# Loading the first tile of a Huber loss kernel in unequal groups of rows

## The chip, the core and the metric

The kernel runs on one core of a Trainium2 chip. Its time is the device time of one execution in microseconds (us); the time before is the median of three runs, 1868.19 us (1867.81 to 1869.9).

## The reference

Two arrays of 8192 x 8192 float32, `pred` and `target`, go in, and the elementwise Huber loss with delta 1 comes out as an array of the same shape.

```python
delta = 1.0
diff = pred - target
abs_diff = np.abs(diff)
return np.where(abs_diff <= delta, 0.5 * diff**2, delta * (abs_diff - 0.5 * delta))
```

The kernel computes it without a choice between branches: with d the difference and c = d clipped to [-1, 1], the loss is the larger of c * c / 2 and |d| - 1/2.

## The kernel before

Each array is taken as one flat row of numbers and cut into 40 blocks. A block is seen as 128 rows, one for each partition of the on-chip memory. `widths` gives the numbers in a row: 7616 in block 0, the remainder, and W = 13248 in the 39 others. `H`, `Q` and `E` are a half, a quarter and an eighth of W.

There are two pairs of buffers, `a_slots` for `pred` and `b_slots` for `target`; block i uses pair i % 2. The schedule is manual: the instructions of each engine stand in the order in which the code writes them. `load(0)` and `load(1)` come first; then, for each block, `compute(i)`, `store(i)` and `load(i + 2)`.

All loads and stores are issued by SyncE (SP in the profile, SPq where its sequencer is meant), so that they go through one queue in one order. In `load`, the inner function `get` (line 53) issues one DMA for some columns of all 128 rows. Blocks 0, 1, n - 3 and n - 2 are loaded in two halves of the columns, `pred` and `target` in turn; the last block in quarters; the others whole. For block 0 that is four DMAs of 128 x 3808 numbers, a row of each being 15232 bytes. `store` (line 70) writes a block from its b buffer, the last block in five pieces.

`compute` takes a block in pieces, block 0 in two halves. VectorE (DVE) subtracts into a (line 92) and clips into b (line 93); ScalarE (ACT) squares b, scaled (line 96), and takes the absolute value of a (line 97); DVE then takes the larger of a - 1/2 and b (line 86, in `finish`, which runs up to two pieces behind). The result stands in b, which `store` reads. So the next load into a buffer waits for ACT, and into b buffer for the store before it.

Of the kernel before, what the change touches and what calls it, by code (L numbers as in the profile page):

```python
# [1 line left out]

# [4 lines left out]


@with_exitstack
def kernel(  # L10
    ctx: ExitStack,
    tc: tile.TileContext,
    pred: bass.AP,
    target: bass.AP,
    out: bass.AP,
):
    nc = tc.nc
    P = 128
    fp32 = mybir.dt.float32
    Alu = mybir.AluOpType  # L20
    Act = mybir.ActivationFunctionType
    SQRT_HALF = 0.70710678118654752

    total = pred.shape[0] * pred.shape[1] // P
    W = 13248
    H, Q, E = W // 2, W // 4, W // 8

    widths = [W] * (total // W)
    if total % W:
        widths.insert(0, total % W)  # L30
    n = len(widths)
    starts = [sum(widths[:i]) * P for i in range(n)]

    def block(x, i):
        flat = x.rearrange("r m -> (r m)")
        return flat[starts[i] : starts[i] + P * widths[i]].rearrange("(p m) -> p m", p=P)

    pool = ctx.enter_context(tc.tile_pool(name="slots", bufs=1))
    a_slots = [pool.tile([P, W], fp32, name=f"a{k}") for k in range(2)]
    b_slots = [pool.tile([P, W], fp32, name=f"b{k}") for k in range(2)]  # L40

    def cuts(pieces):
        at, found = 0, []
        for w in pieces:
            found.append(slice(at, at + w))
            at += w
        return found

    def load(i):
        a, b = a_slots[i % 2], b_slots[i % 2]  # L50

        def get(dst, src, c):
            nc.sync.dma_start(out=dst[:, c], in_=block(src, i)[:, c])  # L53

        if i == n - 1:
            c = cuts([Q] * 4)
            order = [(0, 0), (0, 1), (1, 0), (1, 1), (0, 2), (1, 2), (0, 3), (1, 3)]
            for which, k in order:
                get((a, b)[which], (pred, target)[which], c[k])
            return  # L60
        w = widths[i]
        pieces = [w // 2] * 2 if i in (0, 1, n - 3, n - 2) else [w]
        for c in cuts(pieces):
            get(a, pred, c)
            get(b, target, c)

    def store(i):
        pieces = [Q] * 3 + [E] * 2 if i == n - 1 else [widths[i]]
        for c in cuts(pieces):
            nc.sync.dma_start(out=block(out, i)[:, c], in_=b_slots[i % 2][:, c])  # L70

    def compute(i):
        if i == n - 1:
            pieces = [E] * 8
        elif i == n - 2:
            pieces = [Q] * 4
        elif i == 0:
            pieces = [widths[0] // 2] * 2
        else:
            pieces = [W // 3] * 3  # L80
        todo = []

        def finish(keep):
            while len(todo) > keep:
                a, b = todo.pop(0)
                nc.vector.scalar_tensor_tensor(  # L86
                    out=b, in0=a, scalar=-0.5, in1=b, op0=Alu.add, op1=Alu.max
                )

        for c in cuts(pieces):  # L90
            a, b = a_slots[i % 2][:, c], b_slots[i % 2][:, c]
            nc.vector.tensor_tensor(out=a, in0=a, in1=b, op=Alu.subtract)  # L92
            nc.vector.tensor_scalar(  # L93
                out=b, in0=a, scalar1=-1.0, scalar2=1.0, op0=Alu.max, op1=Alu.min
            )
            nc.scalar.activation(out=b, in_=b, func=Act.Square, scale=SQRT_HALF)  # L96
            nc.scalar.activation(out=a, in_=a, func=Act.Abs)  # L97
            todo.append((a, b))
            finish(2)
        finish(0)  # L100

    ctx.enter_context(tc.manual_schedule())

    load(0)
    load(1)
    for i in range(n):
        compute(i)
        store(i)
        if i + 2 < n:
            load(i + 2)  # L110


# [1 line left out]
_INS = ['pred', 'target']  # L114
_OUTS = [((8192, 8192), 'float32')]


# [23 lines left out]
```

## Time and profile before

| what | value |
|---|---|
| median of 3 runs | 1868.19 us |
| profiled execution, its own time | 1869.17 us |
| its span in the profile | 1867.4 us |
| DVE busy | 1406.2 us, 75% |
| ACT busy | 903.9 us, 48% |
| DMA queue, share of 16 engines | 99.9% |
| bytes read and written | 536.87 MB and 268.44 MB, 431 GB/s over the span |
| DVE L92 waiting for `target` loads | 439.2 us in 42 waits |

The profile shows one execution. The span runs from the first instruction of the program to the last; the profiled execution's own time is 1.77 us longer. "L92" is line 92 of the kernel. A name such as b<-in_target_dram is what is written and what is read. The DMA share is the mean over the core's 16 DMA engines. An idle time in brackets, as in [12.55 <-DMA b<-in_target_dram], is how long the engine had nothing to run before the instruction, and what ended that.

### The profile page before, as it was taken

What the parts mean: (1) busy time and instruction counts of PE and PEld (TensorE: products, weight loads), DVE (VectorE), ACT (ScalarE), POOL (GpSimd) and SP (SyncE); (2) the same over time, 40 slices, a digit from 0 to 9 for tenths busy, and PEclk for the clock granted to TensorE, in tenths of its full rate; (3) what the DMA queues carried; (4) which work ended last, traced back from release to release, by engine and by line L of the source; (5) the groups of instructions that cost most, each with busy time, mean ns of one, the idle gap of its engine ahead of it and who ended that gap; (6) DMA issues with size and microseconds to landing.
All of it is one profiled execution on the core that took longest, in us unless ns stands there. A gap on an engine that the chain in (4) does not pass through costs nothing.

```text
span 1867.4 us, 994 instructions
## 1 busy us (share of the span) xinstructions
DVE 1406.2 (75%) x375; ACT 903.9 (48%) x251; POOL 0.2 (0%) x4
## 2 busy tenths in 40 slices
DVE  5677777777777777777777777777777777777886
ACT  3444444444444444444444444444444444444454
POOL 0000000000000000000000000000000000000000
DMA  9999999999999999999999999999999999999999
GB/s 412 423 432 436 436 431 433 436 432 431 428 435 434 435 432 432 432 435 434 434 434 435 432 434 432 435 434 432 436 434 432 434 434 432 432 436 430 432 429 390
DMA packets 19879, 805.37 MB, mean 431 GB/s; under 512 B 2208, under 2 KB 2208, under 8 KB 2464
## 3 DMA queue, kind: packets, MB, share of 16 engines
q1 hardware_dynamic: 19872, 805.32, 99.9%
q14 instruction: 7, 0.06, 0.0%
HBM read 536.87 MB, written 268.44 MB: 431 GB/s over the span
## 4 chain that ended last, share of the span: by engine, by line
DMA 61%; DVE 37%; issue 0%; SPq 0%; DVEq 0%
DMA b<-in_target_dram 33%; DMA out_dram<-b 28%; DVE b L86 15%; DVE a L92 15%; DVE b L93 8%; SPq L53 0%; DVEq L136 0%; DVEq L92 0%
## 5 line engine op out<-in xcount | busy, mean ns | idle before, releaser
L96 ACT ACTIVATE b<-b 128x4416 f32<-128x4416 f32 (+3 forms) x125 | 461.1, 3688 | 945.6 <-DVE b L93 945.6
L92 DVE TENSOR_TENSOR a<-a,b 128x4416 f32<-128x4416 f32 (+3 forms) x125 | 565.4, 4523 | 439.2 <-DMA b<-in_target_dram 439.2
L86 DVE SCALAR_TENSOR_TENSOR b<-a,b 128x4416 f32<-128x4416 f32 (+3 forms) x125 | 558.6, 4521 | 2.7 <-ACT a L97 2.7
L97 ACT ACTIVATE a<-a 128x4416 f32<-128x4416 f32 (+3 forms) x125 | 460.3, 3682 | 0.0
L93 DVE TENSOR_SCALAR b<-a 128x4416 f32<-128x4416 f32 (+3 forms) x125 | 293.1, 2344 | 4.3
L96 ACT ACT_TABLE_LOAD x1 | 1.3, 1283 | 0.7 <-PEq L125 0.7
L125 POOL MEMSET const-bfloat16-1.0<- 128x1 bf16 x1 | 0.1, 102 | 0.0
L125 POOL MEMSET const-uint8-127<- 128x1 uint8 x1 | 0.1, 101 | 0.0
L125 POOL MEMSET const-float32-0.0<- 128x1 f32 x1 | 0.1, 99 | 0.2 <-issue 0.2
L125 POOL MEMSET const-float32-1.0<- 128x1 f32 x1 | 0.1, 98 | 0.0
## 6 DMA issues: line engine op xcount, KB each, us to landing
out_dram<-b SPq DMA_DIRECT2D x38, 6624.0 KB, 26.9
a<-in_pred_dram SPq DMA_DIRECT2D x35, 6624.0 KB, 42.1
b<-in_target_dram SPq DMA_DIRECT2D x35, 6624.0 KB, 31.3
a<-in_pred_dram SPq DMA_DIRECT2D x6, 3312.0 KB, 30.4
b<-in_target_dram SPq DMA_DIRECT2D x6, 3312.0 KB, 30.5
a<-in_pred_dram SPq DMA_DIRECT2D x4, 1656.0 KB, 31.6
b<-in_target_dram SPq DMA_DIRECT2D x4, 1656.0 KB, 18.6
out_dram<-b SPq DMA_DIRECT2D x3, 1656.0 KB, 18.9
```

Source lines behind the costliest of these rows:

```text
L86: nc.vector.scalar_tensor_tensor(out=b, in0=a, scalar=-0.5, in1=b, op0=Alu.add, op1=Alu.max)
L92: nc.vector.tensor_tensor(out=a, in0=a, in1=b, op=Alu.subtract)
L93: nc.vector.tensor_scalar(out=b, in0=a, scalar1=-1.0, scalar2=1.0, op0=Alu.max, op1=Alu.min)
L96: nc.scalar.activation(out=b, in_=b, func=Act.Square, scale=SQRT_HALF)
L97: nc.scalar.activation(out=a, in_=a, func=Act.Abs)
L125: nc = _bacc.Bacc("TRN2", target_bir_lowering=False, num_devices=1)
```

## The change

The four DMAs of block 0 are each split by rows. The two of `pred` become DMAs of rows 0 to 111, 112 to 125 and 126 to 127; the two of `target` become DMAs of rows 0 to 111, 112 to 121 and 122 to 127. Columns, buffers, the order of the four column pieces, all other loads, the compute and the stores stay as they were. Twelve DMAs are issued in the place of four.

```diff
+    PRED_ROWS = (112, 14, 2)
+    TARG_ROWS = (112, 10, 6)
...
-        def get(dst, src, c):
-            nc.sync.dma_start(out=dst[:, c], in_=block(src, i)[:, c])
+        def get(dst, src, c, rows=(P,)):
+            r = 0
+            for m in rows:
+                nc.sync.dma_start(out=dst[r : r + m, c], in_=block(src, i)[r : r + m, c])
+                r += m
...
-            get(a, pred, c)
-            get(b, target, c)
+            get(a, pred, c, PRED_ROWS if i == 0 else (P,))
+            get(b, target, c, TARG_ROWS if i == 0 else (P,))
```

## The prediction

> **What bounds the kernel.** I read the engine table and the DMA lines of the page first, then the chain, the timeline of the first 60 us, and last the DMA share in the closing microseconds. From the page:
>
> ```profile
> DVE 1406.2 (75%) x375; ACT 903.9 (48%) x251; POOL 0.2 (0%) x4
> DMA 9999999999999999999999999999999999999999
> DMA packets 19879, 805.37 MB, mean 431 GB/s; under 512 B 2208, under 2 KB 2208, under 8 KB 2464
> q1 hardware_dynamic: 19872, 805.32, 99.9%
> DMA 61%; DVE 37%; issue 0%; SPq 0%; DVEq 0%
> ```
>
> No compute engine is near its limit. The DMA share is 9 in every one of the 40 slices, and the one queue's packets fill 99.9% of 16 engines. The program issues 138 DMAs of 128 rows each, and 138 x (128 + 16) = 19872: each row is one packet, and each DMA closes with 16 tiny packets (138 x 16 = 2208, the "under 512 B" count), one for each DMA engine. So an engine carries 8 rows of each DMA. The 37% of DVE in the chain is not a second bound: behind it the DMA queue is never empty. The kernel takes as long as the DMA engine that ends last needs for its own rows and stalls.
>
> The timeline shows the first tile:
>
> ```profile
> 0.73 0.37 SPq L53 DMA_DIRECT2D a<-in_pred_dram  x1
> 1.16 0.42 SPq L53 DMA_DIRECT2D b<-in_target_dram  x1
> ...
> 4.39 0.49 SPq L53 DMA_DIRECT2D b<-in_target_dram  x1
> 12.55 4.12 DVE L92 TENSOR_TENSOR a<-a,b 128x3808 f32<-128x3808 f32 x1 [12.55 <-DMA b<-in_target_dram]
> ...
> 21.62 4.13 DVE L92 TENSOR_TENSOR a<-a,b 128x3808 f32<-128x3808 f32 x1 [2.76 <-DMA b<-in_target_dram]
> ...
> 38.78 0.35 SPq L70 DMA_DIRECT2D out_dram<-b  x1
> ...
> 53.65 4.76 DVE L92 TENSOR_TENSOR a<-a,b 128x4416 f32<-128x4416 f32 x1 [7.73 <-DMA b<-in_target_dram]
> ```
>
> All eight loads are issued by 4.9 us. The two halves of the first tile become ready at 12.55 and 21.62, 9.07 us apart, and a half is two DMAs: 4.53 us for 128 rows, so an engine takes 4.53 / 8 = 0.567 us for a row of 15232 bytes. The first half would be in at 0.73 + 9.07 = 9.80 if the queue had been running; it came at 12.55, so starting from empty costs 2.75 us.
>
> The windows over the end (columns: stretch, length, DVE, ACT and POOL busy, clock, DMA share, GB/s):
>
> ```profile
> 1860.00:1862.00 2.00, 0.00 (x0) 0.00 (x0) 0.00 (x0) 1.00 0.97 401
> 1862.00:1863.00 1.00, 0.00 (x0) 0.00 (x0) 0.00 (x0) 1.00 0.61 252
> 1863.00:1864.00 1.00, 0.00 (x0) 0.00 (x0) 0.00 (x0) 1.00 0.43 179
> 1864.00:1865.00 1.00, 0.00 (x0) 0.00 (x0) 0.00 (x0) 1.00 0.27 113
> 1865.00:1866.00 1.00, 0.00 (x0) 0.00 (x0) 0.00 (x0) 1.00 0.10 40
> ```
>
> The 16 engines do not stop together: they run dry one after another over some 4 us. This unevenness is what uneven first loads could repair. The work left after 1862 is 0.61 + 0.43 + 0.27 + 0.10 = 1.41 us of all 16; shared perfectly it would end at about 1863.5, against about 1866.5 now. No redistribution of rows can gain more than about 3.0 us, or 0.16%.
>
> **The change, part by part.** Bytes, compute instructions and everything after the first tile stay. Four DMAs become twelve.
>
> *Rows per engine.* A 112-row DMA gives each of 16 engines 7 rows. If a small DMA gives an engine at most one row, an engine gets between 28 rows (none of the small ones) and 36 (one from each of the eight), against 32 before: from -4 x 0.567 = -2.3 us to +2.3 us. Which engines are late at the end the profile does not tell (it does not number them), so the sign for the last engine is open. [...]
>
> *Eight more issues on SP.* Each costs 0.37 to 0.65 us. In the built program the DMAs take eight landing semaphores in turn, so that issues 9 to 16 now each wait for the landing of issues 1 to 8; before, the eight initial loads waited for nothing. Behind the waiting issue on SP stand the rest of the first tile and the four loads of the second. When issue 9 waits for the first 112 rows, issues 2 to 8 are in the queue: at least 14 rows or 7.9 us for every engine, against about half a microsecond for an issue. I cost this at nothing; the cover is that backlog, and where it is gone a start from empty costs 2.75 us. Later waits find their semaphores long landed.
>
> *Compute.* DVE gets the first half later by whatever the loads lose. The first store is issued at 38.78 while queued loads last until 53.6: 14.9 us of cover. A loss in the loads moves both ends alike, so the cover stays, and the loss goes to the end of the program unchanged.
>
> *Rows 112 to 127 by themselves.* Here the trace has no row: every DMA of before spans 128 partitions of the tile. Now, four times, 16 neighbouring rows are written alone, by up to 14 engines at once. The lower bound is one row's time, 0.57 us, if the engines don't hinder each other. As the upper bound I take a full piece, 4.53 us, as if the set of 16 cost as much as 128. Likewise the 112 rows cost between 7/8 of a piece, 3.96 us, and a full one, if taking 16 rows off leaves some of what 16 engines write to idle. The sums are 4 x (3.96 + 0.57) = 18.1 us, no change, and 4 x (4.53 + 4.53) = 36.2 us, or +18.1. Nothing in the trace lies nearer to one end, so I take the middle: 4 x (4.53 + 2.27) = 27.2 us, +9.1 us. I don't take the lower end because packets of 16 engines running at one fixed pace, each on its own eight rows, say nothing of fourteen on one small block.
>
> [...]
>
> **The sum.** The profiled execution has a span of 1867.40 and a time of 1869.17, so 1.77 us lie around the span; it is 0.98 above the median 1868.19. Span after: 1867.40 + 9.1 = 1876.5; time 1878.3; median 1877.3.
>
> **Rivals.**
>
> *Evening out (not slower).* If engines don't hinder each other in those 16 rows, only the row counts matter. If the engines that end last are those that get 28 or 30 rows, the last loses 2.3 us, the next ones 1.1, and the early ones take the time over: about 1.9 us gained, 1866.3. If the late engines get the extra rows it is up to 2.3 us lost, 1870.5. It decides where a set of 16 rows costs less than about 1.1 us instead of 2.27. For it: each engine keeps to 0.567 us a row, and the tail of 4 us is of the size that plus or minus 2.3 us makes. Against it: the late engines would have to be the right ones. Either way it stays within 0.2% (3.7 us), which is about what a measurement of this kernel can tell from no change; a gain over that is excluded but for chance, since perfect balance gives 3.0.
>
> *Few rows are not spread.* If a small DMA runs on one or few engines, or 112 rows are spread badly, one engine gets up to 4 x 16 = 64 rows for its four: about +34 us, 1902; a milder case, +18, is the upper end of my own bounds, 1886. For it: only 128-row DMAs have been seen on 16 engines. Against it: 112 is a multiple of 16, and nothing forces the small sets together.
>
> *An empty queue.* The waits of issues 9 to 16 could let some engines run dry if engines drift apart by more than the 7.9 us of backlog. The engines that run dry are the early ones, which lose nothing at the end, so I put 2.75 us as its most, 1871, and little chance.
>
> **How the numbers follow.** Hindrance in the small sets, with +4 to +14 us around +9.1: 0.58. Evening out, within 0.2% either way: 0.26, of which 0.02 for a gain over 0.2%. Not spread: 0.10. A small loss, an empty queue among it, +2.3 to +4: 0.06, some 0.02 of it within 0.2%. So faster 0.02, same 0.26, slower 0.72. The range runs from 1866.6, which takes in most of the second case, to 1884, which takes in the first up to +16; some 0.05 is left out below and 0.12 above. The likeliest case alone has 1872 to 1882.
>
> **What would show it.** Right: the first DVE instruction starts about 4.5 us later (17 instead of 12.55), the second half about 9 us later (31), packets in the first 25 us last longer than one row's usual time and the GB/s of that stretch fall from about 435 to about 300, and from there everything is the old trace moved by 9 us, the tail of uneven engines longer than 4 us. Wrong: the two halves again about 9 us apart, the GB/s unchanged from 4 us on; then the only difference is in the closing microseconds, a steeper fall (gain) or a longer one (loss). If the halves are 9 us or more late each, rows are not spread.

## The result, and the profile after

The changed kernel takes 1885.87 us (median of 5 runs, 1885.58 to 1886.05), the kernel before 1868.15: 17.7 us more, a ratio of 1.0093 with a 95% interval of 1.0078 to 1.0108. The forecast was slower by 9.1 us with a range up to 1884.0, so the direction was right and the size half of the measured one. The profiled execution has a span of 1884.2 us.

From the page of the changed kernel:

```profile
DVE 1406.3 (75%) x375; ACT 903.9 (48%) x251; POOL 0.2 (0%) x4
DMA 9999999999999999999999999999999999999998
GB/s 258 438 434 432 434 432 433 434 434 434 434 433 436 433 433 433 433 433 433 435 434 432 434 434 432 434 436 433 432 435 434 432 434 433 434 433 427 424 423 383
DMA packets 19943, 805.37 MB, mean 427 GB/s; under 512 B 2272, under 2 KB 2272, under 8 KB 2528
q1 hardware_dynamic: 19936, 805.32, 99.8%
```

The compute is the same to 0.1 us. The DMA share is still 9 nearly everywhere, and this is the trap of this profile: the engines look just as busy. What changed is the rate, and nearly all of it in the first of the 40 slices: 258 GB/s, where the same line of the kernel before begins with 412:

```profile
GB/s 412 423 432 436 436 431 433 436 432 431 428 435 434 435 432 432 432 435 434 434 434 435 432 434 432 435 434 432 436 434 432 434 434 432 432 436 430 432 429 390
```

The share counts the time that packets take, however little they move in it: between 15 and 20 us it was 1.12 at 195 GB/s. By the packet records of the two traces, a row of the first tile took a median of 0.57 us before and 0.98 us after.

The count of closing packets says something of how the DMAs were spread. 138 DMAs of 128 rows made 2208 of them before, 16 each; with 16 for each of the 134 DMAs of 128 rows and the 4 of 112 rows it is 138 x 16 = 2208 again. That leaves 2272 - 2208 = 64 = 2 x (14 + 2 + 10 + 6), which is what comes out if each small DMA closes with as many packets as it has rows. So the count speaks for rows that were spread. How many rows of a DMA each engine had, it does not tell.

The timeline of the first tile:

```profile
0.73 1.18 SPq L57 DMA_DIRECT2D a<-in_pred_dram  x3
1.95 1.28 SPq L57 DMA_DIRECT2D b<-in_target_dram  x3
3.27 7.28 SPq L57 DMA_DIRECT2D a<-in_pred_dram  x3
11.46 7.79 SPq L57 DMA_DIRECT2D b<-in_target_dram  x3
...
21.74 4.12 DVE L97 TENSOR_TENSOR a<-a,b 128x3808 f32<-128x3808 f32 x1 [21.74 <-DMA b<-in_target_dram]
...
41.00 4.13 DVE L97 TENSOR_TENSOR a<-a,b 128x3808 f32<-128x3808 f32 x1 [12.96 <-DMA b<-in_target_dram]
...
58.17 0.35 SPq L75 DMA_DIRECT2D out_dram<-b  x1
```

The first half is ready at 21.74 in the place of 12.55 (+9.2), the second at 41.00 in the place of 21.62 (+19.4), and the first store is issued at 58.17 in the place of 38.78 (+19.4). The halves are 19.3 us apart, where they were 9.07. SP's issues stretch because issues 9 to 16 wait for landings, 23.4 us in eight waits.

The windows over the start of the changed kernel, and over its end (columns as before: stretch, length, busy times, clock, DMA share, GB/s):

```profile
4.00:6.00 2.00, 0.00 (x0) 0.00 (x0) 0.00 (x0) 1.00 1.03 289
6.00:8.00 2.00, 0.00 (x0) 0.00 (x0) 0.00 (x0) 1.00 1.01 259
8.00:10.00 2.00, 0.00 (x0) 0.00 (x0) 0.00 (x0) 1.00 1.14 190
10.00:15.00 5.00, 0.00 (x0) 0.00 (x0) 0.00 (x0) 1.00 0.93 274
15.00:20.00 5.00, 0.00 (x0) 0.00 (x0) 0.00 (x0) 1.00 1.12 195
```

```profile
1878.00:1879.00 1.00, 0.00 (x0) 0.00 (x0) 0.00 (x0) 1.00 0.54 225
1879.00:1880.00 1.00, 0.00 (x0) 0.00 (x0) 0.00 (x0) 1.00 0.36 146
1880.00:1881.00 1.00, 0.00 (x0) 0.00 (x0) 0.00 (x0) 1.00 0.26 106
1881.00:1882.00 1.00, 0.00 (x0) 0.00 (x0) 0.00 (x0) 1.00 0.19 79
1882.00:1883.00 1.00, 0.00 (x0) 0.00 (x0) 0.00 (x0) 1.00 0.08 33
```

For comparison, the lowest and the highest stretch of the kernel before between 4 and 15 us:

```profile
6.00:8.00 2.00, 0.00 (x0) 0.00 (x0) 0.00 (x0) 1.00 0.93 396
8.00:10.00 2.00, 0.00 (x0) 0.00 (x0) 0.00 (x0) 1.00 1.08 465
```

From 4 to 20 us the rate is 190 to 289 GB/s at a full DMA share, where the kernel before had 396 to 465. The stretches at 190 and 195 are those in which, by the order of the queue and the landings, most of the small groups move. At the end the engines still run dry one after another, over some 5 us where it was 4; the work left after 1878 is 0.54 + 0.36 + 0.26 + 0.19 + 0.08 = 1.43 us of all 16, as against 1.41 us after 1862 before. The tail was not evened out.

### The profile page after: what moved, and what is told of

It reads as the page before. It is cut to its first block, busy times and chain, and to the rows that moved or that the text cites. A ratio compares the mean times of both kernels' runs of the same rounds, so it can differ in the third digit from the quotient of the medians.

```text
span 1884.2 us, 1010 instructions
## 1 busy us (share of the span) xinstructions
DVE 1406.3 (75%) x375; ACT 903.9 (48%) x251; POOL 0.2 (0%) x4
## 2 busy tenths in 40 slices
DMA packets 19943, 805.37 MB, mean 427 GB/s; under 512 B 2272, under 2 KB 2272, under 8 KB 2528
## 4 chain that ended last, share of the span: by engine, by line
DMA 62%; DVE 37%; issue 0%; SPq 0%; DVEq 0%
DMA b<-in_target_dram 33%; DMA out_dram<-b 28%; DVE b L91 15%; DVE a L97 15%; DVE b L98 7%; DMA a<-in_pred_dram 1%; SPq L57 0%; DVEq L141 0%; DVEq L97 0%
```

## The experiments

Three theories were put against each other. P: rows that lie together in the tile hinder one another. U: unequal loads, or a DMA on fewer than 16 engines, have a price. Q: the number of DMAs and the waits on SP cost the time. All edits concern the first tile. Differences are against the median of the kernel before on the same chip (1868.2 to 1868.4); ratios have their 95% interval. A longer edit is given in short: `x <- y` stands for a DMA that writes x and reads y, and r counts the DMAs of one load.

**Twelve DMAs without a row split.**

```diff
-    PRED_ROWS = (112, 14, 2)      # rows
-    TARG_ROWS = (112, 10, 6)
+    PRED_ROWS = (1270, 1269, 1269)  # columns, all 128 rows in each
+    TARG_ROWS = (1270, 1269, 1269)
```

`get` then steps through the columns instead of the rows.

> Each of the four loads of the first tile is split in three by columns (1270, 1269 and 1269 numbers), all 128 rows in each: twelve DMAs and eight waits on SP as in the changed kernel, but no row split. If the number of DMAs or the waits of issues 9 to 16 cost the time (theory Q), it is slower by about the 17.7 us of the changed kernel. [...]

Measured: +0.6 us, 1.0004 (0.9995 to 1.0013). Twelve issues and eight waits cost nothing that can be measured; Q is out.

**The split without the unequal groups.**

```diff
+    PRED_ROWS = (112, 16)
+    TARG_ROWS = (112, 16)
```

> Rows 0 to 111 and 112 to 127 of both arrays as two DMAs, the 16 rows one for each engine: the split without the unequal groups, eight DMAs in place of twelve. [...] Theory U (unequal loads of the engines): all engines again have 8 rows of each piece, so 0 to +2 us. Theory Q: four DMAs too many instead of eight, about half, +9 us.

Measured: +13.8 us, 1.0077 (1.0062 to 1.0092). With no unequal groups most of the loss stays: U is not the main cause. The other 3.9 us would go with the unequal groups, but the interval of this run and that of the changed kernel (1.0078 to 1.0108) overlap, so the two alone don't settle that part.

**Two halves of 64 rows.**

```diff
+    PRED_ROWS = (64, 64)
+    TARG_ROWS = (64, 64)
```

> Rows 0 to 63 and 64 to 127 as two DMAs each, four rows per engine. [...] Theory U: both halves are evenly spread, 0. Theory Q: eight DMAs, about +9 us, as in the run before it.

Measured: +19.1 us, 1.0104 (1.0089 to 1.0119). That is about what it would be if each half of 64 rows took the 4.53 us of a whole load: 4 x 4.53 = +18.1 us, an estimate from the trace of the kernel before.

**pred alone.**

```diff
+    PRED_ROWS = (112, 14, 2)
+    TARG_ROWS = (P,)
```

> The change for pred alone (112, 14 and 2 rows); target is loaded as before. Theory P: half of the sets, half of the loss, +8 to +10 us. Theory U: engines get 28+8 to 32+4 rows less evenly by half as much, +1 to +9 us. Theory Q: four more DMAs, +9 us. It doesn't tell the theories apart; it tells whether the loss adds up piece by piece.

Measured: +8.1 us, 1.0043 (1.0027 to 1.0060), a little under half of the 17.7.

**Sixteen neighbouring rows, and every eighth row.** In both, a load is eight DMAs of 16 rows, one row for each engine if they are spread as the count of closing packets of the changed kernel suggests.

```diff
+ dst[16 * r : 16 * r + 16, c]  <-  src[16 * r : 16 * r + 16, c]   # the first
+ dst[r:P:8, c]                 <-  src[r:P:8, c]                  # the second
```

> Each load of the first tile as eight DMAs of 16 neighbouring rows, one row per engine: rows 0 to 15, 16 to 31 and so on. Every engine still gets 8 rows of each piece. [...] Rival theory S (any DMA of few rows is slow by itself, some fixed time for each): as slow as the stepped 16 rows of the run beside it.

> The same 32 DMAs of 16 rows, one row per engine, but each takes every eighth row: 0, 8, 16 to 120, then 1, 9 and so on. [...] Theory S: the same as the run beside it.

Measured: neighbouring +45.0 us, 1.0237 (1.0219 to 1.0254); every eighth +17.9 us, 1.0098 (1.0083 to 1.0113). The number of DMAs and rows is the same, and so is the DMA share between 2 and 30 us but for its scatter (0.93 to 1.15 and 0.99 to 1.09); only the places differ. SP's timeline in the run of neighbouring rows:

```profile
0.73 3.63 SPq L57 DMA_DIRECT2D a<-in_pred_dram  x8
4.97 13.77 SPq L57 DMA_DIRECT2D b<-in_target_dram  x8
20.35 13.78 SPq L57 DMA_DIRECT2D a<-in_pred_dram  x8
35.72 0.31 SPq L57 DMA_DIRECT2D b<-in_target_dram  x1
```

From the ninth issue on each waits for the landing of the one eight before it (24 such waits of 32 issues were seen in the run of every eighth row), so the issues show the pace of the sets: eight take 20.35 - 4.97 = 15.38 us, 1.92 us a set, where a row took 0.567 us in the kernel before. In the packet records the sixteen rows of a set start over some 1.1 of these 1.92 us, so rows of two sets are under way together; what one set takes by itself this run does not show.

**Every ninth, and every fourth row.**

```diff
+ dst[r:P:9, c]  <-  src[r:P:9, c]   # nine DMAs: 15, 15 and seven times 14 rows
+ dst[r:P:4, c]  <-  src[r:P:4, c]   # four DMAs of 32 rows
```

> [...] Theory S: 36 DMAs of few rows, more than the runs of 32 beside it; also slow if unequal loads or a DMA on fewer than 16 engines had a price.

> Each load as four DMAs of every fourth row, 32 rows, two per engine. [...] Theory S: sixteen DMAs, half of the loss of the runs of 32.

Measured: every ninth +13.6 us, 1.0073 (1.0058 to 1.0088); every fourth +0.6 us, 1.0003 (0.9993 to 1.0012). So a split by rows can be free. That the rows of a set span the tile is not enough: those of every eighth row span it too and cost 17.9 us. The loss of every ninth row has a cause of its own, which SP's timeline and a window show:

```profile
0.73 7.45 SPq L57 DMA_DIRECT2D a<-in_pred_dram  x9
8.22 7.25 SPq L57 DMA_DIRECT2D b<-in_target_dram  x9
15.52 7.25 SPq L57 DMA_DIRECT2D a<-in_pred_dram  x9
22.82 7.25 SPq L57 DMA_DIRECT2D b<-in_target_dram  x9
```

```profile
10.00:15.00 5.00, 0.00 (x0) 0.00 (x0) 0.00 (x0) 1.00 0.81 268
```

Nine issues take 7.3 us, 0.81 each, without a wait between them, and the DMA share in that time is 0.75 to 0.82: here the engines waited for SP, which 36 issues kept busy to 30 us. That is not all: 0.81 of the usual 432 GB/s would be 350, and the rate is 268, so the rows were also held longer (a median of 0.66 us in the packet records, against 0.57). With both in one run it can't decide between P and U; the run of one such load, further on, was made for that.

**Which side is short.** Four DMAs of 32 rows as in the free run, but with one side changed from every fourth row to 32 neighbouring ones.

```diff
+ dst[32 * r : 32 * r + 32, c]  <-  src[r:P:4, c]                   # the first
+ dst[r:P:4, c]                 <-  src[32 * r : 32 * r + 32, c]   # the second
```

> Four DMAs of 32 rows for each load of the first tile, as in the run of every fourth row that cost nothing, with the same rows of the arrays (every fourth), but put into 32 neighbouring rows of the tile. The first tile's results are thereby stored in other rows than the reference has; the work is the same. It asks which side of the transfer is short. [...] If it is the arrays' side in memory, 0 to +1 us.

> The counterpart: 32 neighbouring rows of the arrays into every fourth row of the tile; the first tile's results are again stored in other rows. Theory P, the tile's side: 0 to +1 us. The arrays' side: +18 us or more.

Measured: neighbouring in the tile +18.5 us, 1.0101 (1.0084 to 1.0118); neighbouring in the arrays +0.9 us, 1.0005 (0.9995 to 1.0014). The windows of the first and of the second:

```profile
10.00:15.00 5.00, 0.00 (x0) 0.00 (x0) 0.00 (x0) 1.00 0.99 210
15.00:20.00 5.00, 0.00 (x0) 0.00 (x0) 0.00 (x0) 1.00 1.00 213
```

```profile
10.00:15.00 5.00, 0.46 (x1) 0.49 (x1) 0.00 (x0) 1.00 1.01 430
15.00:20.00 5.00, 4.97 (x2) 0.79 (x1) 0.00 (x0) 1.00 0.99 424
```

At the same DMA share the rate is 213 and 424 GB/s, half and whole. The packet records say the same: a row took a median of 1.18 us in the first run and 0.57 in the second (1.15 in the run of every eighth row, 1.92 in that of sixteen neighbouring ones). The short side is the tile, not the memory. Halves of 64 rows, every eighth row and 32 neighbouring rows gave nearly the same loss, +19.1, +17.9 and +18.5 us: about the 18.1 us of the four loads once more. What in the tile sets these times, no trace shows.

**A store in halves, and unequal loads on spread rows.**

```diff
+ out[rows, c]  <-  b[rows, c]   for rows 0:64, then 64:128     # the first: store(0), loads as before
+ b[r:P:9, c]   <-  target[r:P:9, c]   for the last load alone  # the second: other loads as before
```

> Loads as before the change; only the store of the first tile is split into rows 0 to 63 and 64 to 127. [...]

> Loads as before the change but for the last of the four, which is nine DMAs of every ninth row (15, 15 and seven times 14), issued while three whole loads are queued, so that SP's 0.8 us for each issue is hidden, which it was not where all four loads were split so (that run was slow by SP's issues, 36 of 0.81 us). [...] Theory P: unequal loads and DMAs on fewer than 16 engines have no price by themselves: 0 to +0.6 us. If they have one: +3 us or more, a quarter of +13.6.

Measured: the store +7.3 us, 1.0040 (1.0025 to 1.0055), most of the +9.07 that twice the time would make (an estimate: the store has the bytes of two loads of 4.53 us); reading the tile in neighbouring rows is slow as writing it is (a row of this store took a median of 2.0 us in the packet records, 1.13 before). The unequal load +1.8 us, 1.0013 (1.0004 to 1.0022): above the 0 to 0.6 of theory P, its interval reaching down to 0.7, and below the 3 of theory U. SP was not hidden in this run as it was meant to be:

```profile
2.10 16.68 SPq L67 DMA_DIRECT2D b<-in_target_dram  x9
18.82 0.53 SPq L53 DMA_DIRECT2D a<-in_pred_dram  x1
```

```profile
18.00:20.00 2.00, 0.65 (x1) 1.32 (x1) 0.00 (x0) 1.00 0.88 358
```

The nine issues, three of which waited for landings (9.3 us in all), held SP until 18.8 us. Only then was the first load of the second tile issued, and the DMA share fell to 0.88. So part of the 1.8 us may be a queue that ran short. That nine groups of 14 and 15 rows load the engines unequally is my estimate; no trace shows it. Whether unequal loads have a price by themselves stays open, up to these 1.8 us on one load of 4.53; they brought no gain.

**The terms one by one.**

```diff
+    PRED_ROWS = (112,)        # the first: rows 112 to 127 of pred not loaded
+    TARG_ROWS = (P,)
...
+    PRED_ROWS = (P,)          # the second
+    TARG_ROWS = (112, 10, 6)
```

> The 112-row DMAs by themselves: pred's first tile is loaded in rows 0 to 111 alone, target's whole. The last 16 rows of pred are left out and the compute of the first tile covers 112 rows. At 7/8 of a load, 3.96 us, it would be faster by 1.1 us; at a full load, 4.53 us, which the prediction took, 0; if 112 rows take the 6.1 us or so that lie between the median landings in the run of 112 and 16 rows, 2 x (6.1 - 4.53) = +3.1 us.

> The change for target alone (112, 10 and 6 rows), pred loaded as before. [...] If the groups' sizes don't matter, +7 to +8 us, as for pred alone or for 16 rows at once.

Measured: 112 rows alone +3.35 us, 1.0017 (1.0008 to 1.0026), so (3.35 / 2) + 4.53 = 6.2 us for a load of 112 rows, more than for 128; what it does to the load behind it is counted in. target alone +13.1 us, 1.0069 (1.0055 to 1.0082), above the 17.7 - 8.1 = 9.6 that it would be if the loss added up load by load, and well above the 6.9 that are half of the run with 112 and 16 rows: here the groups of 10 and 6 rows cost more than 16 at once. 8.1 + 13.1 = 21.2 is more than the 17.7 of both, so the loss does not simply add up.

## Why the prediction was wrong in size

**What was right.** The bound (the DMA engine that ends last), the direction, and one half of the mechanism: the rows 112 to 127 by themselves take longer than a row's 0.567 us (1.8 us as a set of 16, by the estimate below). The loss goes to the end almost unchanged: the first store is 19.4 us late, the end 17.7 us (by the medians). SP's eight issues and waits cost nothing, as the run in three column pieces shows (+0.6). And the place in the tile decides: one side of the transfer, moved from spread to neighbouring rows with nothing else changed, makes +18.5 us of +0.6.

**What failed.** The step "Rows 112 to 127 by themselves", in its term for the 112 rows. I bounded a 112-row load between 3.96 and 4.53 us and took 4.53, on the thought that taking rows off can at worst save nothing. It took 6.2 us, outside the bounds: 4 x (6.2 - 4.53) = +6.7 us, most of the 8.6 us that the forecast lacked. The other 1.9 us lie in the term for the set. It was nearly right for 16 rows at once: 13.8 / 4 - 1.68 = 1.8 us against the 2.27 that I took (1.68 is 3.35 / 2, what a load of 112 rows costs over one of 128). With the unequal groups 17.7 / 4 - 1.68 = 2.75 us are left for it on average. Two DMAs on few rows stand one behind the other there in the place of one; what each of them takes, no run shows by itself.

With those values the sum is 4 x (6.2 + 2.75) = 35.8 us in the place of 18.1, and +17.7. It must come out so, since 2.75 is what the 17.7 leave, and the split between the two terms is no finer than that: it takes the price of 112 rows beside whole loads for their price beside small groups, and the runs of pred and of target alone don't add up to the change. That 112 rows cost more than a full piece was measured by itself. That the sum equals my upper end, +18.1, is by chance: it was made of other terms.

Why 112 rows are slow stays open. A row took a median of 0.57 us where 128 rows were loaded at once, 1.18 in sets of 32 neighbouring rows and 1.92 in sets of 16. If engines hold one another up in the tile, and 112 rows are given out so that they meet there, that would explain the price, but no run shows which engine writes which row.

**The range and the rivals.** My range ended at +16 because I left the upper bound out as part of the rival "Few rows are not spread", at 0.10. As to the small DMAs the count of closing packets speaks against that rival: 64 for 64 rows fits small DMAs that each run on as many engines as they have rows. Its clause that 112 rows may be spread badly is not excluded; it comes nearest to the step that failed. My sign for it, halves that come 9 us or more late, did appear (9.2 for the first, 10.2 more for the second), so that sign could not tell the rivals apart. The DMA share, 0.93 to 1.14 from 4 to 20 us, shows nothing of an empty queue. Evening out is excluded in this form: it needed a set below about 1.1 us, and it was 1.8 to 2.75. With spread rows an unequal load gained nothing either (+1.8 us), and the closing microseconds of the changed kernel show as much unevenness as before: 1.43 us of work against 1.41. Whether another choice of engines could shorten that tail, by the 0.16% that it allows at most, stays open. So does why the groups of 10 and 6 rows cost more beside whole loads of pred (13.1 us) than beside its split ones.

## What to carry to other kernels

Don't cut a DMA by neighbouring rows of the tile when DMA is the bound: here 64 + 64 rows took twice the time of 128 for loads (+19.1 on 18.1 us) and 1.8 times for a store (+7.3 on 9.07), and 112 rows cost more than 128 (6.2 us against 4.53). Cut by columns (+0.6 us, not measurable). Stepped rows can be free too, but the step matters and has to be tried: every fourth row cost +0.6 us, every eighth +17.9, every ninth +13.6, there in part for SP's time for each issue. Read the GB/s beside the DMA share: a full share at half the rate (0.99 at 210 GB/s, with 32 neighbouring rows) was the sign here that each packet was held longer (1.18 us a row against 0.57).

## What the runs showed that I had not expected

A load of 112 rows takes 6.2 us, one of 128 rows 4.53 us. Sixteen neighbouring rows move at 16 x 15232 bytes / 1.92 us = 127 GB/s, with rows of two sets under way together. In the run of every eighth row the rate was 213 to 225 GB/s between 6 and 35 us, about half of the usual 432. Issuing a DMA of 14 or 15 stepped rows kept SP for 0.81 us, where whole loads took 0.37 to 0.65 us.
